# The probabilities of 16 attention heads turned by VectorE in 32x32 blocks and through DRAM, with each head's output two heads behind its scores

## The chip, the core and the metric

One core of one Trainium2 chip runs the whole program in one launch. The metric is the device time of that launch in microseconds (us). TensorE (PE) multiplies, VectorE (DVE) and ScalarE (ACT) do the element work, GpSimd (POOL) takes a few sums, and SyncE (SP) issues every DMA, all on one queue.

## The reference, cut to what matters

Two layers over 512 tokens of width 1024 in float32: retention with 4 heads, then latent attention (MLA) with 16 heads. The change is in the second. The part of it that counts:

```python
q_cat = jnp.concatenate([q_abs, q_rope], axis=-1) * scale
k_cat = jnp.concatenate([c_kv, k_rope], axis=-1)
def attend(args):                                   # one block of 128 queries
    s = jnp.einsum('bqhc,bkc->bhqk', qb, k_cat)
    s = jnp.where(key_idx[None, :] <= q_idx[:, None], s, neg)
    pr = jax.nn.softmax(s, axis=-1)
    return jnp.einsum('bhqk,bkc->bqhc', pr, c_kv)
...
o = jnp.einsum('bshc,chd->bshd', o_lat, w_uv).reshape(B, S, MLA_WIDTH)
return (jax.nn.silu(gate) * o) @ w_out
```

The scores come out with queries on the partitions. The product with the values needs keys on the partitions, so every head's probabilities have to be transposed.

## The kernel before, in words

Everything lies with channels on the partitions and 512 tokens in the free dimension. Each factor of a product is split into a part `hi` (ACT casts it to fp32r, line 88) and a rest `lo` (DVE subtracts, line 89), and each product is three matmuls, hi·hi, hi·lo and lo·hi (`mm3`, lines 97 to 99). Weights arrive raw by DMA (`wraw`, line 109) and are split in the same way (`whi`, `wlo`), in four buffers each.

The loop over 16 MLA heads runs in four groups of four. For head h:

- `mla_scores`: for each of four blocks of 128 queries, five matmuls over 128, 256, 384 or 512 keys into one of four PSUM banks of the pool `s` (three of `hpack` halves, L97 to L99, and two of the rotary part, L580 and L581). A DVE operation (L584) adds the mask and takes the row minimum, ACT takes the exponential with its row sum (L586), DVE the reciprocal (L587) and the scaling (L588). All four blocks lie in one tile `sm`.
- `mla_qk(h+1)`: the next head's queries and keys, 18 and 6 matmuls of 512 columns with their weights, then split into `hpack`. The next scores read it.
- `finish(h-1)`, which is `mla_pv`: twelve matmuls of 512, 384, 256 and 128 columns (`o_mla`), three of each. DVE multiplies the result by the gate `gl`, which comes from DRAM (`ut`, L613), and it is split into `u`.
- `mla_probs`: ten transposes of 128x128 by TensorE (L598) into banks of the same pool `s`, each then split from PSUM by ACT and DVE into `pt`, four pieces a head.
- Once a group: the output projection of the group before (`out_proj`, 96 matmuls of 512) at the group's head 0, the rotary queries of the next group (`mla_rope_q`, 36 of 512) at head 1, its values (`mla_v`, 48 of 256) at head 2.

The order on each engine is made by a scheduler from the order of the program and the buffers of the pools (8 `tmp`, 4 `mm` banks, 4 `s` banks, 2 `qk` tiles, one `sm`, one `pt`). Each engine then works its own list strictly in order.

The change touches `mla_qk`, `mla_scores`, `mla_probs`, `mla_pv` and the loop over heads, and the places of some tiles in memory.

Of the kernel before, what the change touches and what calls it, by code (L numbers as in the profile page):

```python
# [34 lines left out]
PTW = 1664  # L35
# [15 lines left out]
def trunk(ctx, tc, x, p, pos, gains, invf, rmask, smask, ret_in, ret_out, mla_in, uqk, uq_r, uv,  # L51
# [89 lines left out]
    dve.tensor_scalar(gn_h, g_sb[:, GN:GN + 16], 0.5, None, op0=ALU.mult)  # L141

# [136 lines left out]
    def ret_qk(h, i):  # L279
        acc = [mm_bank(), mm_bank()]  # L280
        for m in range(2):
            proj(acc[m], weights(ret_in[12 * h + 2 * i + m], KC, P), xg)
        pack = sb.tile([P, 2, 2, T], F32R, tag="qk", bufs=2, name="qkpack")
        d1, d2 = tmp("rot1"), tmp("rot2")
        rope_pair(acc[0], acc[1], cos_r, sin_r, d1, d2)
        split(pack[:, 0, 0], pack[:, 1, 0], d1)
        split(pack[:, 0, 1], pack[:, 1, 1], d2)
        return pack

    def ret_scores(h, q, k):  # L290
# [4 lines left out]
        at = sb.tile([P, 2 * PTW + 256], F32R, tag="pt", bufs=1, name="at")  # L295
        for j in range(TC):
            i0, n = IST[j], T - IST[j]
            js = slice(j * P, (j + 1) * P)
            s = s_bank("s_ret")
            for c in range(2):  # L300
                mm3(s[:, :n], (k[:, 0, c, js], k[:, 1, c, js]), (q[:, 0, c, i0:], q[:, 1, c, i0:]), c == 0, c == 1)
            a = tmp("a")
            off = h % 2 * 640 + 128 + i0 - j * P
            dve.tensor_tensor(a[:, :n], s[:, :n], masks[0][:, off:off + n], op=ALU.mult)
            at0 = 384 * j + i0
            split(at[:, at0:at0 + n], at[:, PTW + at0:PTW + at0 + n], a[:, :n])
        return at

    def ret_pv(h, at, v, gs):

        ssq = None
        for m in range(4):
            vs = slice(m * P, (m + 1) * P)
            o = mm_bank("o_ret")
            for j in range(TC):
                i0, n, at0 = IST[j], T - IST[j], 384 * j + IST[j]
                mm3(o[:, i0:], (v[0][:, j, vs], v[1][:, j, vs]),
                    (at[:, at0:at0 + n], at[:, PTW + at0:PTW + at0 + n]), j == 0, j == TC - 1)
            ssq = sum_squares(ssq, o, dve if m == 3 else pool)
            dve.tensor_tensor(gs[:, m], o, gs[:, m], op=ALU.mult)  # L320
        r = rstd_columns(ssq, RV)
        ut = big("u")
        u = [(ut[:, m], ut[:, 4 + m]) for m in range(4)]

        def normed():
            row = rstd_rows(r, "gn_row")
            for m in range(4):
                t = tmp("ut")
                dve.scalar_tensor_tensor(t, gs[:, m], gn_h[:, h * 4 + m:h * 4 + m + 1], row, op0=ALU.mult,
                                         op1=ALU.mult)  # L330
# [84 lines left out]
    rbc0 = rstd_rows(r0, "rbc0", "rbc")  # L415
    gs = ret_gate(0)
# [151 lines left out]

    def mla_scores(hh, pack, qs):

        sm = sb.tile([P, 1280], F32, tag="sm", bufs=1, name="sm")
        st = sb.tile([P, 3, TC], F32, tag="st", bufs=2, name="st")
        segs = []
        for i in range(TC):
            n = (i + 1) * P
            w_ = n
            qi = slice(i * P, (i + 1) * P)
            s = s_bank("s_mla")
            mm3(s[:, :w_], (pack[:, 0, qi], pack[:, 1, qi]), (pack[:, 2, :w_], pack[:, 3, :w_]), True, False)
            pe.matmul(s[:, :w_], qs[:, hh, qi], kr_hi[:, :w_], start=False, stop=False)  # L580
            pe.matmul(s[:, :w_], qs[:, hh, qi], kr_lo[:, :w_], start=False, stop=True)  # L581
            seg = sm[:, seg_at[i]:seg_at[i] + n]
            segs.append(seg)
            dve.tensor_tensor_reduce(seg, s[:, :n], smask_sb[:, T - n:], q_scale[:, i:i + 1], 3e38, ALU.add, ALU.min,  # L584
                                     st[:, 0, i:i + 1])
            act.activation(seg, seg, AF.Exp, bias=st[:, 0, i:i + 1], scale=-1.0, accum_out=st[:, 1, i:i + 1])  # L586
            dve.reciprocal(st[:, 2, i:i + 1], st[:, 1, i:i + 1])  # L587
            dve.tensor_scalar(seg, seg, st[:, 2, i:i + 1], None, op0=ALU.mult)  # L588
        return segs

    def mla_probs(segs):

        pt = sb.tile([P, 2 * PTW + 256], F32R, tag="pt", bufs=1, name="pt")
        for i in range(TC):
            n = (i + 1) * P
            tp = s_bank("tp_p")
            for j in range(i + 1):
                pe.transpose(tp[:, j * P:(j + 1) * P], segs[i][:, j * P:(j + 1) * P], ident)  # L598
            src = tp[:, :n].rearrange("p (j f) -> p j f", f=P)
            split(query_blocks(pt, 0, i), query_blocks(pt, 1, i), src)  # L600
        return pt

    def mla_pv(h, pt, v, dst):
        o = mm_bank("o_mla")
        for j in range(TC):
            i0, n, a0 = IST[j], T - IST[j], 384 * j + IST[j]
            vs = slice(h % 2 * P, h % 2 * P + P)
            mm3(o[:, i0:], (v[:, j, vs], v[:, 4 + j, vs]), (pt[:, a0:a0 + n], pt[:, PTW + a0:PTW + a0 + n]),
# [4 lines left out]
        dve.tensor_tensor(ut, o, gl, op=ALU.mult)  # L613
# [8 lines left out]
    v = mla_v(0)  # L622
# [6 lines left out]
    u = pt = None  # L629
    ssq, add = y_squares()  # L630

    def finish(h):
# [11 lines left out]
        mla_pv(h, pt, vs[grp][hh // 2], u[hh])  # L644

    vs = [v]
    for h in range(MH):
        grp, hh = divmod(h, 4)
        segs = mla_scores(hh, pack, qs)
# [11 lines left out]
        if h in (MH - 3, MH - 2):  # L661
            out_proj(mla_out[8:12], u_prev, y1, (hh,))
        if hh == 1 and grp < 3:
            qs_next = mla_rope_q(grp + 1)
        if hh == 2 and grp < 3:
            vs.append(mla_v(grp + 1))
# [97 lines left out]
```

## Time and profile before

| | |
|---|---|
| median of 3 runs | 1006.53 us (1005.63 to 1006.87) |
| the profiled execution | 1006.76 us, of which the span is 1005.0 and 1.8 lie around it |
| PE busy | 989.6 us of the span, 98% |
| DVE, ACT, POOL busy | 635.7, 413.2 and 68.4 us (63%, 41%, 7%) |
| granted TensorE clock | 1.00 in every stretch of the span |
| the loop over MLA heads | 629.9 to 923 us of the span |

Matmuls are pipelined: one starts before the one ahead has ended, so the time that a matmul takes from PE is read from start to start in the timeline, not from its duration. DVE's operations overlap too, by some 0.07 to 0.10 us. A share of an engine over the whole span says little about one stretch, so the windows over a stretch stand beside it.

### The profile page before, as it was taken

Reading aid. Unit: us, or ns where it says so; the run is one execution under the profiler, and the core shown is the slowest. Engines: PE = TensorE matmul, PEld = TensorE weight load, DVE = VectorE, ACT = ScalarE, POOL = GpSimd, SP = SyncE. Lnnn points to the kernel's source line nnn. Section 1 sums busy time; section 2 is a strip of 40 time slices with the busy share of each in tenths; the row PEclk is TensorE's granted clock in tenths of the full one; section 3 lists DMA queues with packets and bytes.
Section 4 is the critical chain, followed back from the end, with each engine's and each line's share of the span. In section 5 each row is a group of like instructions: output and inputs, shape, how many; then the busy total and the mean of one; then the engine's idle time right before and its main releaser. Section 6 shows DMA issues by size and latency. Waiting matters only on the chain.

```text
span 1005.0 us, 12505 instructions
## 1 busy us (share of the span) xinstructions
PE 989.6 (98%) x4780; PEld 828.6 (82%) x4780; DVE 635.7 (63%) x1062; ACT 413.2 (41%) x683; POOL 68.4 (7%) x54
## 2 busy tenths in 40 slices
PE   6999999999999999999999999999999999999998
PEld 4888888888888888877888888898888889888777
DVE  5776558455645567587664455777377568775583
ACT  6332334333223334555433233655445246444441
POOL 3000100010001002302130000000000000000400
PEclk9999999999999999999999999999999999999999
DMA  6433222412322232444334445342323224221431
GB/s 241 152 86 103 64 84 85 131 63 84 104 84 63 84 89 85 150 139 160 92 94 136 134 136 153 114 135 68 90 75 116 85 76 124 84 99 60 138 103 52
DMA packets 37547, 105.96 MB, mean 105 GB/s; under 512 B 5104, under 2 KB 5872, under 8 KB 37488
## 3 DMA queue, kind: packets, MB, share of 16 engines
q1 hardware_dynamic: 37488, 105.17, 33.9%
q8 instruction: 37, 0.61, 0.2%
q14 instruction: 22, 0.18, 0.1%
HBM read 92.57 MB, written 8.39 MB: 100 GB/s over the span
## 4 chain that ended last, share of the span: by engine, by line
PE 92%; DVE 3%; issue 2%; ACT 1%; DMA 1%; SPq 0%; POOL 0%; POOLq 0%; DVEq 0%; ACTq 0%
PE acc L98 20%; PE acc L99 20%; PE acc L97 20%; PE gate L98 6%; PE gate L99 6%; PE gate L97 6%; PE tp_p L598 1%; PE s_mla L97 1%; PE o_ret L99 1%; PE s_mla L581 1%; PE o_ret L98 1%; PE s_mla L99 1%; PE s_mla L580 1%; PE s_mla L98 1%; PE o_ret L97 1%
## 5 line engine op out<-in xcount | busy, mean ns | idle before, releaser
L88 ACT CAST whi<-wraw 128x1024 fp32r<-128x1024 f32 (+2 forms) x156 | 159.8, 1025 | 343.9 <-PE acc L98 145.7
L89 DVE TENSOR_TENSOR wlo<-wraw,whi 128x1024 fp32r<-128x1024 f32 (+2 forms) x156 | 187.9, 1206 | 89.7 <-ACT whi L88 89.6
L152 POOL TENSOR_TENSOR ssq<-ssq,sq 128x512 f32<-128x512 f32 x38 | 56.3, 1482 | 836.0 <-ACT sq L151 430.5
L97 PE MATMUL gate<-xg_hi,whi 128*128 128x512 f32 x256 | 101.1, 395 | 6.9 <-ACT whi L88 5.6
L98 PE MATMUL gate<-xg_lo,whi 128*128 128x512 f32 x256 | 100.8, 395 | 2.1 <-DVE xg_lo L92 2.1
L99 PE MATMUL gate<-xg_hi,wlo 128*128 128x512 f32 x256 | 100.4, 393 | 0.1
L97 PE MATMUL acc<-u,whi 128*128 128x512 f32 x240 | 93.9, 392 | 0.0
L98 PE MATMUL acc<-u,whi 128*128 128x512 f32 x240 | 93.6, 391 | 0.0
L99 PE MATMUL acc<-u,wlo 128*128 128x512 f32 x240 | 93.5, 390 | 0.0
L97 PE MATMUL acc<-xg_hi,whi 128*128 128x512 f32 x200 | 78.2, 391 | 0.3 <-ACT xg_hi L91 0.3
L98 PE MATMUL acc<-xg_lo,whi 128*128 128x512 f32 x200 | 78.0, 390 | 0.3 <-DVE xg_lo L92 0.3
L99 PE MATMUL acc<-xg_hi,wlo 128*128 128x512 f32 x200 | 77.9, 389 | 0.0
L97 PE MATMUL acc<-c_hi,whi 128*128 128x512 f32 x176 | 69.2, 393 | 0.0
L251 DVE TENSOR_TENSOR g<-gate,rbc 128x512 f32<-128x512 f32 x32 | 22.0, 690 | 74.0 <-PE gate L99 74.0
L99 PE MATMUL acc<-c_hi,wlo 128*128 128x512 f32 x176 | 68.8, 391 | 0.0
L98 PE MATMUL acc<-c_lo,whi 128*128 128x512 f32 x176 | 68.7, 390 | 0.0
L346 DVE TENSOR_TENSOR y<-acc,y 128x512 f32<-128x512 f32 x48 | 33.1, 691 | 51.2 <-PE acc L99 51.2
L97 PEld LDWEIGHTS gate<-xg_hi,whi 128*128 128x128 f32 x256 | 48.4, 189 | 18.1 <-ACT whi L88 6.3
L98 PEld LDWEIGHTS gate<-xg_lo,whi 128*128 128x128 f32 x256 | 48.4, 189 | 14.0 <-DVE xg_lo L92 4.1
L99 PEld LDWEIGHTS gate<-xg_hi,wlo 128*128 128x128 f32 x256 | 48.4, 189 | 10.3 <-DVE wlo L89 0.4
L98 PEld LDWEIGHTS acc<-u,whi 128*128 128x128 f32 x240 | 45.1, 188 | 9.8 <-DVE u L89 0.5
L97 PEld LDWEIGHTS acc<-u,whi 128*128 128x128 f32 x240 | 45.1, 188 | 9.3
(195 smaller groups left out, 2074.9 us busy)
## 6 DMA issues: line engine op xcount, KB each, us to landing
wraw<-in_ret_in SPq DMA_DIRECT2D x47, 512.0 KB, 3.6
wraw<-in_mla_in SPq DMA_DIRECT2D x25, 512.0 KB, 3.7
wraw<-in_ret_out SPq DMA_DIRECT2D x16, 512.0 KB, 3.6
wraw<-in_ple_g SPq DMA_DIRECT2D x16, 512.0 KB, 3.6
wraw<-in_uqk SPq DMA_DIRECT2D x16, 512.0 KB, 3.8
wraw<-in_mla_out SPq DMA_DIRECT2D x16, 512.0 KB, 3.7
gs_dram<-gsl SPq DMA_DIRECT2D x16, 256.0 KB, 4.1
qs<-rq SPq DMA_DIRECT2D x64, 64.0 KB, 2.0
```

The source lines that it names most:

```text
L88: act.copy(hi, src)
L89: dve.tensor_tensor(lo, src, r32(hi), op=ALU.subtract)
L97: pe.matmul(acc, ah, bh, start=first, stop=False)
L98: pe.matmul(acc, ah, bl, start=False, stop=False)
L99: pe.matmul(acc, al, bh, start=False, stop=last)
L152: (eng or pool).tensor_tensor(acc, acc, sq, op=ALU.add)
L251: dve.tensor_tensor(g, acc, rbc, op=ALU.mult)
L346: dve.tensor_tensor(y[:, c], acc, y[:, c], op=ALU.add)
L580: pe.matmul(s[:, :w_], qs[:, hh, qi], kr_hi[:, :w_], start=False, stop=False)
L581: pe.matmul(s[:, :w_], qs[:, hh, qi], kr_lo[:, :w_], start=False, stop=True)
L598: pe.transpose(tp[:, j * P:(j + 1) * P], segs[i][:, j * P:(j + 1) * P], ident)
```

## The change

`mla_scores` no longer keeps its blocks in `sm`: each block has a tile of the pool `tmp` (`seg`), and after the scaling DVE transposes each 128x128 piece in 32x32 blocks (ten STREAM_TRANSPOSE of 128x4x32 a head) into `tr`, which now has the one buffer of `sm`. `mla_fetch` stores `tr` (640 KB) to DRAM and loads it back with four DMAs of 32 partitions each (160 KB), which puts the blocks in their places, into `raw`, one buffer. `mla_probs` splits `raw` from SBUF in two pieces instead of four from PSUM. The queries of a head now lie as 4x32 interleaved pieces: the matmuls of `mla_pv` write `oq[:, :, 32j:]`, four pieces of up to 128 columns, and the multiplication by the gate puts them in natural order. TensorE's ten transposes a head are gone.

The output of a head comes two heads behind (`finish(h-2)`) and its probabilities one behind. `mla_v` moves to the group's head 0 for that group, `out_proj` to head 1, and the pieces of the last ones go behind the last scores. The retention's `at` and the heads' `hpack` lie elsewhere: `at` is packed to 1280 columns, and halves of `hpack` and `qkpack` start 64 columns apart from a multiple of 512; three unused tiles (`pad`) shift what follows them.

```diff
     def ret_qk(h, i):
...
-        pack = sb.tile([P, 2, 2, T], F32R, tag="qk", bufs=2, name="qkpack")
+        pack = sb.tile([P, QK], F32R, tag="qk", bufs=2, name="qkpack")
+        pack = pack[:, i * 64:i * 64 + 4 * T].rearrange("p (a c t) -> p a c t", a=2, c=2)
...
     def mla_qk(h):
-        pack = sb.tile([P, 4, T], F32R, tag="qk", bufs=2, name="hpack")
+        flat = sb.tile([P, QK], F32R, tag="qk", bufs=2, name="hpack")
+        pack = [flat[:, at:at + T] for at in (0, T, 2 * T + 64, 3 * T + 64)]
...
     def mla_scores(hh, pack, qs):
...
-        sm = sb.tile([P, 1280], F32, tag="sm", bufs=1, name="sm")
+        tr = sb.tile([P, 4, NS // 4], F32, tag="sm", bufs=1, name="tr")
...
-            seg = sm[:, seg_at[i]:seg_at[i] + n]
+            seg = tmp("seg")
...
-            dve.tensor_scalar(seg, seg, st[:, 2, i:i + 1], None, op0=ALU.mult)
+            dve.tensor_scalar(seg[:, :n], seg[:, :n], st[:, 2, i:i + 1], None, op0=ALU.mult)
             for j in range(i + 1):
-                pe.transpose(tp[:, j * P:(j + 1) * P], segs[i][:, j * P:(j + 1) * P], ident)
-            src = tp[:, :n].rearrange("p (j f) -> p j f", f=P)
-            split(query_blocks(pt, 0, i), query_blocks(pt, 1, i), src)
+                at = 32 * (JST[j] + i - j)
+                dve.transpose(tr[:, :, at:at + 32], seg[:, j * P:(j + 1) * P].rearrange("p (b k) -> p b k", k=32))
+        return tr
+
+    def mla_fetch(h, tr):
+
+        sp.dma_start(pt_dram[h], tr)
+        raw = sb.tile([P, 4, NS // 4], F32, tag="ptraw", bufs=1, name="raw")
+        for b in range(4):
+            sp.dma_start(raw[b * 32:(b + 1) * 32], pt_dram[h, :, b].rearrange("(a k) f -> k a f", k=32))
+        return raw
+
+    def mla_probs(raw):
+
+        pt = sb.tile([P, 2, 4, NS // 4], F32R, tag="pt", bufs=1, name="pt")
+        for at in (slice(0, 128), slice(128, NS // 4)):
+            split(pt[:, 0, :, at], pt[:, 1, :, at], raw[:, :, at])
         return pt
 
     def mla_pv(h, pt, v, dst):
         o = mm_bank("o_mla")
+        oq = o.rearrange("p (a q) -> p a q", a=4)
         for j in range(TC):
-            i0, n, a0 = IST[j], T - IST[j], 384 * j + IST[j]
+            at = slice(32 * JST[j], 32 * (JST[j] + TC - j))
...
-            mm3(o[:, i0:], (v[:, j, vs], v[:, 4 + j, vs]), (pt[:, a0:a0 + n], pt[:, PTW + a0:PTW + a0 + n]),
+            mm3(oq[:, :, 32 * j:], (v[:, j, vs], v[:, 4 + j, vs]), (pt[:, 0, :, at], pt[:, 1, :, at]),
...
     for h in range(MH):
...
+        if hh == 0:
+            vs.append(mla_v(grp))
         if h == MH - 1:
-            out_proj(mla_out[8:12], u_prev, y1, (3,))
-            ple = ple_proj(1, ple_input(1))
+            out_proj(mla_out[8:12], u_prev, y1, (1,))
+        if h > 1:
+            finish(h - 2)
         if h:
-            finish(h - 1)
-        pt = mla_probs(segs)
-        if hh == 0 and grp:
+            pts[h - 1] = mla_probs(raw)
+        raw = mla_fetch(h, tr)
+        if hh == 1 and grp:
...
+    ple = ple_proj(1, ple_input(1))
+    out_proj(mla_out[8:12], u_prev, y1, (2,))
+    finish(MH - 2)
+    pts[MH - 1] = mla_probs(raw)
+    out_proj(mla_out[8:12], u_prev, y1, (3,))
     next(ple)
     finish(MH - 1)
```

What the scheduler makes of it. On PE, from the end of head 3's pass to head 4's scores (`o_mla` is an output, of head 2 before and of head 1 in the change; `acc<-c_hi` is the projection for head 5; `s_mla` are head 4's scores), before:

```order
L99 MATMUL o_mla<-pt,v_4613 128x128
L598 MATMUL tp_p<-ident,sm 128x128 x10
L97 MATMUL acc<-c_hi,whi 128x512
L98 MATMUL acc<-c_lo,whi 128x512
L97 MATMUL s_mla<-hpack 128x128
L98 MATMUL s_mla<-hpack 128x128
L99 MATMUL s_mla<-hpack 128x128
```

and in the change:

```order
L106 MATMUL o_mla<-pt,v_4871 128x4x32
L104 MATMUL s_mla<-hpack 128x128
L104 MATMUL s_mla<-hpack 128x256
L104 MATMUL s_mla<-hpack 128x384
L104 MATMUL s_mla<-hpack 128x512
L104 MATMUL acc<-c_hi,whi 128x512
L105 MATMUL acc<-c_lo,whi 128x512
L106 MATMUL acc<-c_hi,wlo 128x512
L104 MATMUL acc<-c_hi,whi 128x512
L105 MATMUL acc<-c_lo,whi 128x512
L105 MATMUL s_mla<-hpack 128x128
L106 MATMUL s_mla<-hpack 128x128
```

The transposes are gone; the four hi·hi products of the scores, which need no `lo` of `hpack`, and five matmuls of the next projection now stand ahead of the first product that reads the `lo` of the keys.

On DVE, in head 3 (tile numbers tell heads apart: `hpack_5375` before and `hpack_5307` in the change are head 4's queries and keys), before:

```order
L588 TENSOR_SCALAR sm_5333<-sm_5333,st_5334 128x384
L587 RECIPROCAL st_5334<-st_5334 128x1
L588 TENSOR_SCALAR sm_5333<-sm_5333,st_5334 128x512
L89 TENSOR_TENSOR hpack_5375<-acc_5382,hpack_5375 128x512
L89 TENSOR_TENSOR wlo_5645<-wraw_5643,whi_5644 128x1024
L89 TENSOR_TENSOR hpack_5375<-acc_5403,hpack_5375 128x512
L613 TENSOR_TENSOR ut1_5427<-o_mla_5412,gl_5425 128x512
L89 TENSOR_TENSOR pt_5431<-tp_p_5432,pt_5431 128x128
```

and in the change (`hpack_5430` is head 5's, `raw_5246` head 2's probabilities, `o_mla_5344` head 1's output):

```order
L602 STREAM_TRANSPOSE tr_5251<-seg_5271 128x4x32 x2
L599 TENSOR_SCALAR seg_5284<-seg_5284,st_5252 128x384
L598 RECIPROCAL st_5252<-st_5252 128x1
L96 TENSOR_TENSOR hpack_5307<-acc_5335,hpack_5307 128x512
L602 STREAM_TRANSPOSE tr_5251<-seg_5284 128x4x32 x3
L599 TENSOR_SCALAR seg_5298<-seg_5298,st_5252 128x512
L96 TENSOR_TENSOR wlo_5690<-wraw_5688,whi_5689 128x1024
L602 STREAM_TRANSPOSE tr_5251<-seg_5298 128x4x32 x4
L96 TENSOR_TENSOR hpack_5430<-acc_5437,hpack_5430 128x512
L96 TENSOR_TENSOR pt_5363<-raw_5246,pt_5363 128x4x128
L632 TENSOR_TENSOR ut1_5359<-o_mla_5344,gl_5357 128x512
```

The second `lo` half of head 4's `hpack` now stands behind the reciprocal of the 512-key block, and the last four transposes, the multiplication by the gate and the split of head 2's probabilities around a projection of head 5. On ACT the exponentials of the 384- and 512-key blocks, which stood ahead of both copies of `hpack`, now stand behind them, with a weight cast between the two. On SP each head now has `gl`, the store of `tr` (it waits for DVE's last transpose), two weight loads, and the four loads into `raw` (they wait for the store to land and for the readers of `raw`), in this order.

## Rows read from the trace of the kernel before

**Rows 1.** The page's first part: span; busy us, share and instructions by engine.

```profile
span 1005.0 us, 12505 instructions
...
PE 989.6 (98%) x4780; PEld 828.6 (82%) x4780; DVE 635.7 (63%) x1062; ACT 413.2 (41%) x683; POOL 68.4 (7%) x54
```

**Rows 2.** Windows: stretch, us, busy PE, PEld, DVE, ACT, POOL, clock, DMA share, GB/s.

```profile
629.90:923.00 293.10, 292.73 (x1589) 254.72 (x1588) 201.33 (x474) 144.82 (x306) 0.00 (x0) 1.00 0.31 95
660.00:677.30 17.30, 17.30 (x116) 15.99 (x115) 15.54 (x36) 10.40 (x22) 0.00 (x0) 1.00 0.49 154
```

**Rows 3.** PE's timeline, 689 to 701: start, duration, engine, line, operation, tiles.

```profile
689.12 0.40 PE L98 MATMUL acc<-c_lo,whi 128*128 128x512 f32 x1
689.63 0.33 PE L97 MATMUL s_mla<-hpack 128*128 128x128 f32 x1
...
692.93 0.39 PE L99 MATMUL acc<-c_hi,wlo 128*128 128x512 f32 x1
...
697.72 0.40 PE L99 MATMUL acc<-c_hi,wlo 128*128 128x512 f32 x1
697.95 0.39 PE L97 MATMUL o_mla<-pt,v 128*128 128x512 f32 x1
...
699.81 1.28 PE L598 MATMUL tp_p<-ident,sm 128*128 128x128 f32 x10
700.85 0.47 PE L97 MATMUL acc<-u,whi 128*128 128x512 f32 x1
```

**Rows 4.** The chain of waits, 684 to 690: start, us, what.

```profile
688.10 0.68 DVE hpack L89
688.78 0.60 DVE ut L613
```

**Rows 5.** DVE groups by form, 629.9 to 923: busy us, mean ns | idle before.

```profile
L89 DVE TENSOR_TENSOR wlo<-wraw,whi 128x1024 fp32r<-128x1024 f32 x32 | 39.2, 1223 | 21.1 <-ACT whi L88 21.1
L89 DVE TENSOR_TENSOR hpack<-acc,hpack 128x512 fp32r<-128x512 f32 x30 | 20.6, 686 | 16.4 <-ACT hpack L88 16.4
...
L587 DVE RECIPROCAL st<-st 128x1 f32<-128x1 f32 x64 | 9.8, 159 | 4.4 <-ACT sm L586 4.0
...
L89 DVE TENSOR_TENSOR pt<-tp_p,pt 128x256 fp32r<-128x256 f32 x16 | 6.6, 415 | 0.0
...
L89 DVE TENSOR_TENSOR wlo<-wraw,whi 128x768 fp32r<-128x768 f32 x5 | 4.8, 958 | 8.5 <-ACT whi L88 8.5
...
L588 DVE TENSOR_SCALAR sm<-sm,st 128x128 f32<-128x128 f32 x16 | 4.4, 278 | 0.1
```

**Rows 6.** DVE's timeline, one head's softmax, 691 to 696.

```profile
691.49 0.34 DVE L584 CUSTOM_DVE_ANT_0 sm<-s_mla,smask_sb,q_scale 128x128 f32<-128x128 f32 x1
...
695.08 0.17 DVE L587 RECIPROCAL st<-st 128x1 f32<-128x1 f32 x1 [0.35 <-ACT sm L586]
695.28 0.49 DVE L588 TENSOR_SCALAR sm<-sm,st 128x512 f32<-128x512 f32 x1
```

**Rows 7.** ACT groups by form, 629.9 to 923.

```profile
L88 ACT CAST whi<-wraw 128x1024 fp32r<-128x1024 f32 x32 | 33.7, 1053 | 46.9 <-PE acc L98 42.0 <-issue 4.9
...
L586 ACT ACTIVATE sm<-sm,st 128x512 f32<-128x512 f32 x16 | 11.6, 726 | 8.2 <-DVE st L584 8.2
L586 ACT ACTIVATE sm<-sm,st 128x384 f32<-128x384 f32 x16 | 9.9, 618 | 5.6 <-DVE st L584 5.6
```

**Rows 8.** PE groups by form, 629.9 to 923.

```profile
L97 PE MATMUL s_mla<-hpack 128*128 128x256 f32 x16 | 5.3, 333 | 0.0
...
L98 PE MATMUL s_mla<-hpack 128*128 128x256 f32 x16 | 4.4, 277 | 0.0
```

**Rows 9.** The view of DMA issues: count, KB each, median us from issue to landing.

```profile
gs_dram<-gsl SPq DMA_DIRECT2D x16, 256.0 KB, 4.1
...
masks<-in_rmask SPq DMA_DIRECT2D x2, 640.0 KB, 5.1
```

**Rows 10.** SP's timeline, 744 to 755: sixteen loads in one row.

```profile
744.87 10.02 SPq L534 DMA_DIRECT2D qs<-rq  x16
```

More of the change, by code (lines that the diff above doesn't have):

```diff
@@ L33 @@
 IST = (0, 128, 256, 384)
-PTW = 1664
+JST = (0, 4, 7, 9)
+NS = 1280
+QK = 4 * T + 128
 WG = 1024
@@ L61, in trunk, with pad @@
     gs_dram = dr.tile([MH, P, T], F32, name="gs_dram")
+    pt_dram = dr.tile([MH, P, 4, NS // 4], F32, name="pt_dram")
+    def pad(name, n):
+        sb.tile([P, n], F32, name=name)
     def r32(ap):
@@ L294, in ret_scores @@
             sp.dma_start(masks[0], rmask[h // 2])
-        at = sb.tile([P, 2 * PTW + 256], F32R, tag="pt", bufs=1, name="at")
+        if h == 0:
+            pad("pad_pt", 64)
+        at = sb.tile([P, 2, NS], F32R, tag="pt", bufs=1, name="at")
         for j in range(TC):
@@ L304, in ret_scores @@
             dve.tensor_tensor(a[:, :n], s[:, :n], masks[0][:, off:off + n], op=ALU.mult)
-            at0 = 384 * j + i0
-            split(at[:, at0:at0 + n], at[:, PTW + at0:PTW + at0 + n], a[:, :n])
+            at0 = JST[j] * P
+            split(at[:, 0, at0:at0 + n], at[:, 1, at0:at0 + n], a[:, :n])
         return at
@@ L415, in trunk @@
     rbc0 = rstd_rows(r0, "rbc0", "rbc")
+    pad("pad_g8", 120)
     gs = ret_gate(0)
@@ L560, in mla_qk @@
         proj(acc, wq, cq)
-        split(pack[:, 0], pack[:, 1], acc)
+        split(pack[0], pack[1], acc)
         acc = mm_bank()
         proj(acc, lambda c, i, m: wq(6 + c, i, m), ckv)
-        split(pack[:, 2], pack[:, 3], acc)
+        split(pack[2], pack[3], acc)
         return pack
-    seg_at = (0, 128, 384, 768)
     def mla_scores(hh, pack, qs):
-        sm = sb.tile([P, 1280], F32, tag="sm", bufs=1, name="sm")
+        tr = sb.tile([P, 4, NS // 4], F32, tag="sm", bufs=1, name="tr")
@@ L589, in mla_scores @@
[L589 to L596, printed above, removed]
-            for j in range(i + 1):
-                pe.transpose(tp[:, j * P:(j + 1) * P], segs[i][:, j * P:(j + 1) * P], ident)
-            src = tp[:, :n].rearrange("p (j f) -> p j f", f=P)
-            split(query_blocks(pt, 0, i), query_blocks(pt, 1, i), src)
+            mm3(s[:, :n], (pack[0][:, qi], pack[1][:, qi]), (pack[2][:, :n], pack[3][:, :n]), True, False)
@@ new lines, in mla_scores @@
+            pe.matmul(s[:, :n], qs[:, hh, qi], kr_hi[:, :n], start=False, stop=False)
+            pe.matmul(s[:, :n], qs[:, hh, qi], kr_lo[:, :n], start=False, stop=True)
+            seg = tmp("seg")
+            dve.tensor_tensor_reduce(seg[:, :n], s[:, :n], smask_sb[:, T - n:], q_scale[:, i:i + 1], 3e38, ALU.add,
+                                     ALU.min, st[:, 0, i:i + 1])
+            act.activation(seg[:, :n], seg[:, :n], AF.Exp, bias=st[:, 0, i:i + 1], scale=-1.0,
+                           accum_out=st[:, 1, i:i + 1])
@@ L612, in mla_pv @@
         ut = tmp("ut1")
[L613 removed]
+        natural = lambda t: t.rearrange("p (i a q) -> p i a q", i=TC, a=4)
+        dve.tensor_tensor(natural(ut), o.rearrange("p (a i q) -> p i a q", i=TC, a=4), natural(gl), op=ALU.mult)
         split(*dst, ut)
@@ L621, in trunk @@
     qs = mla_rope_q(0)
-    v = mla_v(0)
     pack = mla_qk(0)
@@ L628, in trunk @@
     y1 = big("y1", F32)
-    u = pt = None
+    u, vs, pts, raw = None, [], {}, None
     ssq, add = y_squares()
@@ L643, in finish @@
             u += [(ut[:, m], ut[:, 2 + m]) for m in range(2)]
[L644 to L646 removed]
+        mla_pv(h, pts[h], vs[grp][hh // 2], u[hh])
     for h in range(MH):
         grp, hh = divmod(h, 4)
[L649 removed]
+        tr = mla_scores(hh, pack, qs)
         if h + 1 < MH:
             pack = mla_qk(h + 1)
+        if hh == 0:
+            vs.append(mla_v(grp))
         if h == MH - 1:
[L653 to L654 removed]
+            out_proj(mla_out[8:12], u_prev, y1, (1,))
+        if h > 1:
+            finish(h - 2)
         if h:
[L656 to L658 removed]
+            pts[h - 1] = mla_probs(raw)
+        raw = mla_fetch(h, tr)
+        if hh == 1 and grp:
             u_prev = u
             out_proj(mla_out[4 * (grp - 1):4 * grp], u, y1, range(4) if grp < 3 else (0,), first=grp == 1)
[L661 to L662 removed]
         if hh == 1 and grp < 3:
             qs_next = mla_rope_q(grp + 1)
[L665 to L666 removed]
         if hh == 3 and grp < 3:
             qs = qs_next
+    ple = ple_proj(1, ple_input(1))
[3 more added lines that the diff above has]
+    out_proj(mla_out[8:12], u_prev, y1, (3,))
     next(ple)
```

17 lines of the change are left out of this document (3 added, 14 removed).

## The prediction, made before the run

> **What bounds the kernel now.** First the shares: PE is busy 98% of the span, DVE 63% [rows 1]. Then the windows, since the change works between 629.9 and 923: there PE is busy 292.7 of 293.1 us at clock 1.00, DVE 201.3 and ACT 144.8 [rows 2]. PE is the bound, and what leaves PE comes off the time as long as no other engine then makes PE wait. DVE comes next, and its 69% is an average: in its fullest stretch, 17.3 us from 660, it is busy 15.54 us, 90% [rows 2]. PE's timeline gives the true price of its work, from start to start, and the one place where it waits: after 689.12 a matmul of 512 columns should pass in 0.23, but the next starts 0.51 later, at 689.63 [rows 3], a wait of 0.28. The chain of waits names the cause: DVE makes a `lo` half of `hpack`, then the gated output, and PE follows [rows 4]. This stands at the end of three groups' third heads, 0.85 us in all. The profiled execution took 1006.76, 0.2 above the median of 1006.53; the sum below starts from the former.
>
> **What PE loses.** A head's ten transposes take PE from 699.81 to 700.85 [rows 3], 1.04 us; 16 heads make **16.6 us**, all of it on the path.
>
> **What PE does in a head.** Scores 689.63 to 692.93, 3.30; a projection matmul (697.95−692.93)/22 = 0.228, so 24 take 5.48; the output 697.95 to 699.81, 1.86 [rows 3]. Together 10.64 us without the transposes. The places of `hpack` may also help a little: of two matmuls of the same form, that on the `hi` keys is 56 ns longer than that on the `lo` keys [rows 8]; 16 of them make 0.9. With the like in other forms I bound this by 0 and 2 us and take **0.5**.
>
> **What DVE gets.** Splitting four pieces from PSUM becomes two from SBUF, of 512 and 768 elements. The nearest rows, 686 and 958 ns [rows 5], less 0.08 of overlap each, give 1.48 us a head. New are ten transposes of 128 elements a partition. No row shows one. The cheapest small operation is a reciprocal of one element, 159 ns; a row that surely does more is a split of 256 elements, 415 ns. The nearest in work is the scaling of 128 elements from SBUF, 278 ns [rows 5], 0.20 from start to start. I take **0.20**, 2.0 us a head, and keep 0.15 to 0.42, 1.5 to 4.2 a head. The Trainium skill (VectorE: DVE Perf Modes, The three transpose paths) gives 311 ns for a 128x128 bf16 transpose on VectorE and 390 on TensorE, and advises TensorE where its result may go to PSUM; by that an operation would come every 0.23, 0.3 a head more, and the sum below would be between nothing and 3.6 us worse (1.2 in each of three groups).
>
> The softmax of a head runs from 691.49 to 695.77 with 0.35 idle [rows 6], 3.85 us. Two `hpack` halves at 0.61, the gated output and its split at 0.61 each (all like the 686 ns row) make 2.44. With 1.48 and 2.0 a head costs DVE **9.77 us** against PE's 10.64: it fits, barely. But PE's list has heads 2 to 5 with little beside them: four heads, 42.6, and `mla_v`, 48 matmuls of half the columns at 0.12, 5.8, together 48.4 us. DVE has there 39.1, the splits of `v` (four at 0.61, 2.4) and six weight splits at 1.15 (1223 ns less 0.08 [rows 5]), 6.9: also 48.4. Two full engines that feed each other can't both run without waits.
>
> **The wait that takes the place.** I walk head 3 to head 4, with zero where PE starts head 3's scores. The projection's first accumulator is ready at 3.3 + 18 × 0.228 = 7.4, the second at 8.8. ACT copies both by about 9.5, then does the 384-key exponential (618 ns and the row sum, 0.8), a weight cast (1053 ns) and the 512-key exponential (726 and 0.19) [rows 7], which end at 10.3, 11.35 and 12.3. DVE's reciprocal, 12.4, stands ahead of the second `lo` half in its list, so that half is ready at 13.1. PE, after 10.64, does the four hi·hi products of the next scores (0.63) and five matmuls of the next projection (1.14), and wants the half at 12.4: it waits 0.7. Walked alike: 0.95 from head 2 to 3; 1.4 from 4 to 5, where DVE's list holds the splits of head 2's probabilities and the gated output behind a projection of head 5, so that the mask of the last block, and with it a bank of `s`, comes late; 0.6 in head 5's output projection, which wants `u` of head 3. That is **3.65 a group**, three groups, and 0.95 from head 14 to 15: 11.9, of which I leave 0.6 to slack in the output projection of the third group, which is cut in pieces: **11.3**. The 0.85 of today goes, since those heads' ends are walked anew: **+10.4**.
>
> **Edits at nothing.** ACT has less to cast (two pieces for four) and has 148 us idle in the stage [rows 2]. The store of 640 KB takes about the 5.1 us of the masks' load, at least the 4.1 of 256 KB [rows 9]; the four loads cost SP 4 × 0.63 (10.02/16 [rows 10]) and land some 4 later. From a head's last transpose, some 14 us after its scores began, store (5.1), loads (2.5 to issue, 4 to land) and split (1.5) end at 27; its output starts at 2 × 10.64 + 8.8 = 30. SP stands at the store until DVE's last transpose and at the loads until the store has landed, and the next weights stand behind both; they are loaded a head ahead of use, with four buffers. `tr` has one buffer: the next head's first transpose waits until the store has read it. I walk 5.6 to 6.2 us between a head's last transpose and the next one's first, against 0.4 + 5.1. Thin, hence a rival below. After head 15 PE has 22 us of output projection, gate and head 14's output ahead of the last output, which needs 17: covered. If it were not, 2 to 4 us would show once.
>
> **Sum.** 1006.8 − 16.6 − 0.5 + 10.4 = 1000.1, so **1000.0 us**, by itself 995 to 1004.5.
>
> **Rivals.**
> - *The waits are covered.* The scheduler's list lets PE run ahead by a projection (24 × 0.228) and a delay of one head may be made up in the next; for it speaks that today's DVE, 90% full, costs PE 0.85 us only [rows 2, 3], against it the equal sums of 48.4. Then 1006.8 − 16.6 − 0.5 = 989.7, with up to 2 for the places of the tiles 988.2. Chance 0.28.
> - *DVE becomes the bound: slower.* If a transpose comes every 0.42, as for 256 elements [rows 5], a head costs 2.2 more; four heads 8.8, of which DVE's idle time beside my waits takes 3.6, leaves 5.2 a group, 15.7 and once 2.2 more: 1018. The tie is where 40(c − 0.20) − 3.6 a group, three times, and 10(c − 0.20) once make 6.7: c = 0.34. For it: the operation moves columns to partitions, which no row does, and a scaling of 128 is the best case. Against it: it has one SBUF input and few elements. Chance 0.17, a third of it within 0.2% of today.
> - *The output's matmuls write in pieces.* They write PSUM as four pieces of 96, 64 or 32 columns, nine of twelve with gaps; those nine take 1.86 − 3 × 0.23 = 1.17 us a head today [rows 3]. Twice that would add 18.7: 1018.8. No matmul of the trace writes with gaps, so the trace neither shows nor excludes it. The Trainium skill (SBUF — State Buffer, the box on SBUF cachelines) says that non-contiguous PSUM access slows matmuls much, as PSUM's lines hold two fp32 values; runs of 32 columns and more cross a line no more often than one long run, so I give the case little: chance 0.04.
> - *The store comes late.* If it lands 6.5 after its issue instead of 5.1, DVE stands about 1 us at ten heads' first transposes, with reciprocals and `hpack` halves behind; hidden in part, +6: 1006. Chance 0.06.
>
> **How the numbers follow.** Forecast 0.45, covered 0.28, DVE dear 0.17, pieces 0.04, store late 0.06. A measurement of this kernel can tell 0.2%, 2 us, from no change: 1004.5 to 1008.5 count as the same. Faster: 0.45 + 0.28 = 0.73. Same: 0.06 and a third of 0.17, 0.12. Slower: the rest, 0.15. The range runs from the covered case, 988.5, to the dear transpose as far as c = 0.36, 1010; outside stay about 0.03 below and 0.13 above.
>
> **What would show it.** 160 STREAM_TRANSPOSE on DVE, from start to start near 0.20; no matmul of `tp_p`; PE's idle time before `s_mla` on `hpack` released by DVE, 0.5 to 1.5 us at the ends of heads 2, 3 and 4 of each group and none in the output projections' bulk; DVE in heads 2 to 5 busy over 95%; output matmuls still 0.23, 0.17, 0.13 and 0.11 apart; no wait of DVE on the store of `tr`. I am wrong if the transposes come over 0.34 apart, if ACT waits for the loads into `raw`, or if PE stays over 99% busy through the dense heads.

## The result and the profile after

The changed kernel takes **995.38 us** (median of 4 runs, 995.32 to 996.77), against 1006.61 for the kernel before in the same session: a ratio of 0.9893 with a 95% interval of 0.9881 to 0.9905, 11.2 us less. Predicted were 1000.0 (988.5 to 1010) and 0.73 for faster. The direction was right, the size too small: 6.5 us forecast, 11.2 measured.

The first part of the page answers to [rows 1]:

```profile
span 993.5 us, 12481 instructions
...
PE 973.0 (98%) x4620; PEld 812.3 (82%) x4620; DVE 658.2 (66%) x1190; ACT 405.0 (41%) x651; POOL 68.4 (7%) x54
```

The span is 11.5 us shorter. PE is busy 16.6 us less and idle 5.1 more (20.5 against 15.4), so part of what was gained came back as waits. The 16.6 is not the price of the transposes alone: it also holds what the tiles' places gave (run 1), and a 512-column matmul counts as busy for 0.39 us but passes in 0.23, so the first part of each wait counts as busy too. DVE gained 128 instructions and 22.5 us. Now DVE's groups in the MLA loop (operation, shape, count | busy us, mean ns | idle before):

```profile
L602 DVE STREAM_TRANSPOSE tr<-seg 128x128 f32<-128x128 f32 x160 | 37.0, 280 | 0.1
L96 DVE TENSOR_TENSOR pt<-raw,pt 128x768 fp32r<-128x768 f32 x16 | 15.2, 948 | 0.0
L96 DVE TENSOR_TENSOR pt<-raw,pt 128x512 fp32r<-128x512 f32 x16 | 10.8, 675 | 0.8 <-ACT pt L95 0.8
```

A block transpose takes 280 ns, the same as the scaling of as many elements, 278 [rows 5]. From start to start it is 0.20 us, as DVE's timeline in head 2 shows: four transposes take 0.81 us to the start of the next operation, three take 0.61.

```profile
664.57 0.68 DVE L602 STREAM_TRANSPOSE tr<-seg 128x128 f32<-128x128 f32 x3
665.18 0.44 DVE L599 TENSOR_SCALAR seg<-seg,st 128x512 f32<-128x512 f32 x1
...
666.14 0.88 DVE L602 STREAM_TRANSPOSE tr<-seg 128x128 f32<-128x128 f32 x4
666.95 1.51 DVE L96 TENSOR_TENSOR pt<-raw,pt 128x512 fp32r<-128x512 f32 x2
```

(37.0 / 160 = 0.23 is more, since it counts the last transpose of every run in full, with the part that overlaps the next operation. The expectations of runs 2 and 9 below use that 0.23.) The transpose almost never waits: 0.1 us idle in front of 160 of them, so `tr`'s single buffer holds nobody up. The windows over heads 2 to 5 show where DVE's new work bites (columns as in [rows 2]):

```profile
654.70:665.20 10.50, 10.50 (x58) 9.21 (x56) 10.25 (x31) 6.71 (x14) 0.00 (x0) 1.00 0.26 65
665.20:676.50 11.30, 10.83 (x59) 9.28 (x58) 8.90 (x27) 5.10 (x12) 0.00 (x0) 1.00 0.80 240
676.50:689.80 13.30, 13.27 (x83) 11.74 (x82) 9.48 (x28) 6.64 (x15) 0.00 (x0) 1.00 0.64 194
689.80:711.30 21.50, 20.55 (x109) 17.52 (x108) 21.50 (x63) 11.62 (x25) 0.00 (x0) 1.00 0.66 184
```

DVE is idle 3.8 of 13.3 us in the third stretch and then full, 21.5 of 21.5, in the fourth, where PE waits most. DVE's timeline at the seam shows why (the bracket is the idle time before and who ended it):

```profile
680.46 0.88 DVE L602 STREAM_TRANSPOSE tr<-seg 128x128 f32<-128x128 f32 x4
684.93 0.69 DVE L96 TENSOR_TENSOR hpack<-acc,hpack 128x512 fp32r<-128x512 f32 x1 [3.59 <-ACT hpack L95]
685.54 0.68 DVE L96 TENSOR_TENSOR pt<-raw,pt 128x512 fp32r<-128x512 f32 x1
686.13 0.68 DVE L632 TENSOR_TENSOR ut<-o_mla,gl 128x512 f32<-128x512 f32 x1
```

ACT's timeline at the same place:

```profile
684.31 0.59 ACT L95 CAST hpack<-acc 128x512 fp32r<-128x512 f32 x1 [6.66 <-PE acc L106]
684.79 1.36 ACT L95 CAST pt<-raw 128x512 fp32r<-128x512 f32 x2
```

and SP's, with the store of head 2 and its loads:

```profile
668.65 0.40 SPq L607 DMA_DIRECT2D pt_dram<-tr  x1
...
672.98 1.75 SPq L610 DMA_DIRECT2D raw<-pt_dram  x4
```

The loads into `raw` for head 2 are issued from 672.98 to 674.73 and land some 4 us after the last issue (the median of these loads is 4.0 us), before 680. ACT, with nothing to do from 677.7, and DVE from 681.3 both stand at a copy of head 5's projection, which PE finishes at 684.3. The split of `raw`, the gated output and its split are ready and queue behind it; DVE does them when the next head's masks are due as well. PE's timeline has the bill at the same place:

```profile
689.78 0.58 PE L104 MATMUL s_mla<-hpack 128*128 128x128 f32 x3
690.68 0.49 PE L104 MATMUL s_mla<-hpack 128*128 128x512 f32 x1 [0.32 <-DVE st L594]
691.80 0.38 PE L104 MATMUL acc<-whi,c_hi 128*128 128x256 f32 x1 [0.62 <-DVE hpack L96]
```

From start to start these two gaps cost 0.54 and 1.00 us beyond the matmuls' own time, the second with 0.10 for the slower start of the matmul behind it. In the first PE waits for a bank of `s` that DVE's mask still reads, in the second `mla_v`, which reads no `hpack`, waits for the accumulator bank that DVE's subtraction for `hpack` still reads. Counted so, all gaps over 0.25 us in the loop are: heads 2 to 3 and 3 to 4 of the first group 0.69 and 0.30; the groups' first heads (4, 8, 12) 1.54, 2.17 and 1.41; 0.28 and 0.34 elsewhere; 0.57 before head 15's scores; 1.57 in front of the last output. Together 8.9, where before there were 0.85. Those at heads 4, 8 and 12 are 5.1 of it.

### The profile page after: what moved, and what is told of

Read it like the earlier page. It is cut to its first block, busy times and chain, and to the rows that moved or that the text cites. A ratio compares the mean times of both kernels' runs of the same rounds, so it can differ in the third digit from the quotient of the medians.

```text
span 993.5 us, 12481 instructions
## 1 busy us (share of the span) xinstructions
PE 973.0 (98%) x4620; PEld 812.3 (82%) x4620; DVE 658.2 (66%) x1190; ACT 405.0 (41%) x651; POOL 68.4 (7%) x54
## 4 chain that ended last, share of the span: by engine, by line
PE 88%; DVE 6%; issue 2%; ACT 2%; DMA 1%; SPq 0%; POOL 0%; POOLq 0%; DVEq 0%; ACTq 0%
PE acc L105 20%; PE acc L104 19%; PE acc L106 19%; PE gate L105 6%; PE gate L106 6%; PE gate L104 6%; PE s_mla L105 1%; PE o_ret L105 1%; PE o_ret L106 1%; PE o_ret L104 1%; PE s_mla L106 1%; PE s_mla L592 1%; PE s_mla L591 1%; PE o_mla L105 1%; PE o_mla L106 1%
## 5 line engine op out<-in xcount | busy, mean ns | idle before, releaser
L106 PEld LDWEIGHTS acc<-u,wlo 128*128 128x128 f32 x240 | 45.1, 188 | 9.4
L105 PEld LDWEIGHTS acc<-u,whi 128*128 128x128 f32 x240 | 45.1, 188 | 9.4 <-DVE u L96 0.2
```

The costliest lines, as they stand in the source:

```text
L105: pe.matmul(acc, ah, bl, start=False, stop=False)
L106: pe.matmul(acc, al, bh, start=False, stop=last)
```

## The experiments

Theory A: the gain is the ten transposes off PE's path, and what comes back is made by the order of ACT's and DVE's lists, which put work that is ready behind a copy that isn't. Rival B: by DVE's load. Rival C: by the trip through DRAM. A further question was the price of the tiles' places. Medians are compared with the changed kernel's 995.38; ratios, where given, are to the kernel before, whose medians were 1006.34 to 1006.61 in every session. In some runs the granted clock fell after waits of PE. What that cost is estimated from the mean granted clock of the profiled span, as the part of the span that is missing from full speed: 1.0 us for the changed kernel (0.999 of 993.5).

**1. The places of the tiles undone.**

```diff
-QK = 4 * T + 128
+QK = 4 * T
...
-    pad("pad_ssq", 104)
...
-        pack = pack[:, i * 64:i * 64 + 4 * T].rearrange("p (a c t) -> p a c t", a=2, c=2)
+        pack = pack[:, 0:4 * T].rearrange("p (a c t) -> p a c t", a=2, c=2)
...
-            pad("pad_pt", 64)
...
-    pad("pad_g8", 120)
...
-        pack = [flat[:, at:at + T] for at in (0, T, 2 * T + 64, 3 * T + 64)]
+        pack = [flat[:, at:at + T] for at in (0, T, 2 * T, 3 * T)]
```

> The changed kernel with hpack and qkpack back at multiples of 512 columns and the three unused tiles taken out; nothing else differs. Theory A (the gain is the ten transposes off TensorE, less new waits of PE on DVE; the places of the tiles are worth about 1 us): 996 to 997 us, and the hi*hi and rotary score matmuls a few ns longer from start to start. Rival B (the places carry a good part of the 11 us gained): 999 us or more.

Measured 998.46 (996.68 to 999.38, 5 runs), ratio 0.9919 (0.9905 to 0.9932); span 995.4 against 993.5. So the places are worth 1.9 us by the profiled spans, 3.1 by the medians; this kernel's runs spread with a granted clock of 0.997 to 1.000. PE is busy 975.8 us here, only 13.8 less than before:

```profile
PE 975.8 (98%) x4620; PEld 811.9 (82%) x4620; DVE 658.3 (66%) x1190; ACT 404.9 (41%) x651; POOL 68.3 (7%) x54
```

It isn't `hpack`: the pair of [rows 8] is unmoved by the places (the product on the `lo` keys took 277 ns before and takes some 309 with either places). In the changed kernel, with the 64-column offsets:

```profile
L105 PE MATMUL acc<-x_lo,whi 128*128 128x512 f32 x120 | 46.3, 393 | 0.5 <-DVE x_lo L96 0.5
...
L104 PE MATMUL acc<-x_hi,whi 128*128 128x512 f32 x120 | 44.8, 391 | 0.4 <-ACT x_hi L95 0.4
L104 PE MATMUL s_mla<-hpack 128*128 128x256 f32 x16 | 5.3, 334 | 0.0
L105 PE MATMUL s_mla<-hpack 128*128 128x256 f32 x16 | 5.0, 309 | 0.0
```

and with the places undone:

```profile
L105 PE MATMUL acc<-x_lo,whi 128*128 128x512 f32 x120 | 46.7, 396 | 0.3 <-DVE x_lo L96 0.3
L104 PE MATMUL acc<-x_hi,whi 128*128 128x512 f32 x120 | 45.4, 396 | 0.3 <-ACT x_hi L95 0.3
L104 PE MATMUL s_mla<-hpack 128*128 128x256 f32 x16 | 5.3, 333 | 0.0
L105 PE MATMUL s_mla<-hpack 128*128 128x256 f32 x16 | 4.9, 308 | 0.0
```

The gate matmuls of the two tails, on `x_hi` and `x_lo`, take 3 to 5 ns less each with the places as changed: 360 of them, 1.4 us. Whether the unused tiles or the offsets do it was not taken apart. The median lies between what the two theories expected: the places carry more than A said, but 2 to 3 of the 11 us, not most of them.

**2. Every block transpose twice.**

```diff
-                dve.transpose(tr[:, :, at:at + 32], ...)
+                for _ in range(2):
+                    dve.transpose(tr[:, :, at:at + 32], ...)
```

> Every block transpose of VectorE is issued twice, so a head costs DVE ten more at 0.23 us, 2.3 us. From head 2 to head 6 of the first group the changed kernel has DVE busy about 50 of 57 us. Theory A (the waits that are left are PE waiting for DVE in the dense heads): four heads bring 9.2 us a group against some 6.5 of idle time, part of which the list can't use; three groups and one head more: 10 to 25 us slower, 1005 to 1020, with PE's waits on hpack, the gate and the masks' banks growing. Rival B (DVE has slack, the waits come from the trip through DRAM): at most 3 us slower, below 999.

Measured 1005.25 (10 runs), ratio 0.9984 (0.9975 to 0.9993): 9.9 us slower than the changed kernel, the mild end of theory A, for 30.1 us more on DVE (busy 688.3 us against 658.2; 160 more at 0.20 make 32). DVE was busy 55.0 of 59 us from 656 to 715, and the granted clock stayed at 1.00. DVE's load matters, at about a third of its amount.

**3. Splits of the probabilities ahead of the projection's copy.**

```diff
-    def mla_qk(h):
+    def mla_qk(h, after=None):
...
-        split(pack[0], pack[1], acc)
+        if after:
+            with tc.issue_after(after[0].ins), tc.issue_after(after[1].ins):
+                split(pack[0], pack[1], acc)
+        else:
+            split(pack[0], pack[1], acc)
```

> The changed kernel, but at the first head of a group the split of the earlier head's probabilities is put ahead of the copy of the next projection's first half, on ACT and on DVE. In the changed kernel both engines stand idle 3 to 3.6 us at that place, for a projection, with the loaded probabilities behind it, and PE then waits 1.5, 2.2 and 1.4 us in heads 4, 8 and 12. Theory A (head-of-line: the order of the list, not DVE's capacity, makes these waits): they fall by half or more, 990.5 to 993. Rival B (DVE is simply full there, 21.5 of 21.5 us): within 1 us of 995.4. Rival C (the loads land later than the projection): ACT waits for the load and it is slower, 996 to 999.

Measured 1002.16 (5 runs), 6.8 us slower, and for none of the three reasons. The splits did run early (DVE at 681.1), but ACT's list now had the cast of `u` behind the copies of the projection, and DVE and the masks behind that: the same fault in another place, as DVE's timeline shows.

```profile
683.09 0.34 DVE L598 CUSTOM_DVE_ANT_0 seg<-s_mla,smask_sb,q_scale 128x128 f32<-128x128 f32 x1
...
686.60 0.69 DVE L96 TENSOR_TENSOR u<-ut,u 128x512 fp32r<-128x512 f32 x1 [3.15 <-ACT u L95]
```

ACT does wait 2.60 us for the load there, as rival C has it, but ends the split before the projection is ready. PE's waits grew, with one of 2.1 us at each of heads 8 and 12, and the granted clock fell after heads 4 and 8; its mean, 0.996 of 1000.4 us, makes some 3 of the 6.8 us, an estimate.

**4. Loads that don't wait for the store.**

```diff
-            sp.dma_start(raw[b * 32:(b + 1) * 32], pt_dram[h, :, b]...)
+            src = rmask[0].rearrange("p (b f) -> p b f", b=4)
+            sp.dma_start(raw[b * 32:(b + 1) * 32], src[:, b]...)
```

> The loads into raw read a constant table of the same size in DRAM and so don't wait for the store of the transposed probabilities; the store is still made. The attention uses that table in place of the probabilities. Theory A (the trip through DRAM is covered by the lag of two heads, except after the last head): PE's waits in the groups stay, only the 1.6 us before the last head's output go: 993.5 to 995.5. Rival C (store and load set the waits in heads 2 to 5 too): those go as well, below 992.

Measured 991.94 (4 runs), ratio 0.9857 (0.9843 to 0.987): theory A missed. The waits at heads 4, 8 and 12 shrank to 0.55 each, and the one before the last output, which A gave to the trip, stayed. This looked like rival C, but the edit had also changed the lists: since the loads no longer depend on the store, the scheduler put the splits of `pt` and of `u` ahead of the projection's copies by itself. Run 5 takes the two apart.

**5. That order with the real loads.** At each group's first head both halves of the next projection's split, the values' splits and the later weights are held behind what is ready:

```diff
+            pack = mla_qk(h + 1, (list(last), [exps[1]]) if h and hh == 0 else ((), ()))
...
+            late = [exps[3]] if h else []
+            vs.append(mla_v(grp, late))
```

(`last` holds the last splits of `u` and `pt`, `exps` the exponentials.)

> The same question as the run that put only the split of the probabilities ahead and was slower: there ACT's cast of u fell behind the projection's copies, and DVE and PE behind it. Here, at the first head of groups 1 to 3, all that is ready stands ahead: split of the probabilities, split of u, then the first half of the next projection, the exponentials, the second half, the values; real loads. It is nearly the list that the run with free loads had by itself. Theory A (order of the lists): 991.5 to 993, the waits at heads 4, 8 and 12 down to about 0.6 each. Rival C (the trip through DRAM sets them): ACT waits for the loads, 995 or more.

Measured **992.52** (992.3 to 992.82, 4 runs), ratio 0.9861 (0.9845 to 0.9877): 2.9 us below the changed kernel and the best version of this study. The trip through DRAM was not the limit; the order was. ACT's timeline at the same seam as above:

```profile
679.33 1.36 ACT L101 CAST pt<-raw 128x512 fp32r<-128x512 f32 x2 [1.40 <-DMA raw<-pt_dram]
682.83 0.62 ACT L101 CAST u<-ut 128x512 fp32r<-128x512 f32 x1 [2.15 <-DVE ut L641]
684.58 0.59 ACT L101 CAST hpack<-acc 128x512 fp32r<-128x512 f32 x1 [1.13 <-PE acc L112]
```

and DVE's:

```profile
681.54 0.65 DVE L102 TENSOR_TENSOR pt<-raw,pt 128x512 fp32r<-128x512 f32 x1
...
683.58 0.69 DVE L102 TENSOR_TENSOR u<-ut,u 128x512 fp32r<-128x512 f32 x1
```

ACT splits at 679.33, as soon as the load has landed, instead of 684.79; DVE has done all of it by 684.2, where it used to begin. PE's gaps at heads 4 and 8 fell from 1.54 and 2.17 to 0.55 each; at head 12 they rose from 1.41 to 2.0, which was not followed up. The wait of 1.57 before the last output went too, as PE's list there now puts matmuls of the next projection between those of the output. Against that, PE now waits some 0.7 us at the end of each group's third head, and in the changed kernel only in the first group.

**6. The last head as well.** As run 5, with the third and fourth weight casts of the last projection behind the last split of `pt`.

```diff
+    out_proj(mla_out[12:16], u, y1, (0, 1), on_chunk=add)
+    with behind(last_pt):
+        out_proj(mla_out[12:16], u, y1, (2, 3), on_chunk=add)
```

> As the run before, and the casts of the last projection's third and fourth weights stand behind the split of the last head's probabilities. In the changed kernel and with free loads PE waits 1.6 us before the last head's output, and ACT holds that split behind a weight cast that waits for PE. Theory A: 1 to 1.6 us less than the run before, 990 to 992. Rival C (the last head's trip sets it): the same as the run before, within 0.5.

992.84 (4 runs), the same: run 5 had already lost that wait, with PE doing part of the next projection there, so this run had nothing left to show.

**7. `u`'s rest on GpSimd.** As run 6, and

```diff
-        last[:2] = split(*dst, ut)
+        last[:2] = (act.copy(dst[0], ut), pool.tensor_tensor(dst[1], ut, r32(dst[0]), op=ALU.subtract))
```

> As the run before, with the subtraction that makes u's lo part on GpSimd, which is idle there (its 128x512 sums take about 1.5 us each), and DVE 0.6 us a head lighter. Theory A (DVE close to full in the dense heads, but what is left of the waits, about 0.6 at four or five places, comes from the order of copy, exponential and lo half): 0 to 2 us less. Rival D (GpSimd and DVE slow each other on SBUF): slower by 1 us or more, DVE's operations longer.

995.59 (993.52 to 995.9, 4 runs): no gain, rather a loss. DVE's operations are not longer (block transposes 284 ns against 285 in run 6, the split of `raw` 954 against 955), so there is no sign of rival D. One gap of PE behind DVE's `hpack` at head 12 grew to 2.1 us. The profile is of the fastest execution, 993.52, at a granted clock of 0.999; the other three, 995.29 to 995.90, show 0.998, and where their time went isn't shown. Taking 0.6 us a head from DVE brought nothing.

**8. One head behind.**

```diff
-        if h > 1:
-            finish(h - 2)
         if h:
             pts[h - 1] = mla_probs(raw)
+            finish(h - 1)
         raw = mla_fetch(h, tr)
-        if hh == 1 and grp:
+        if hh == 0 and grp:
...
-    finish(MH - 2)
```

(So `out_proj` is back at head 0.)

> The changed kernel with a head's output one head behind its scores, and the output projection one head earlier, as before. Theory A (the lag covers store, loads and split): a head's loads land some 24 us after its scores began (head 2: 654.7 to about 679) and its split ends 2.5 later, while its output would come some 19 to 20 after: 5 to 8 us of PE waiting in the heads that have nothing else beside them, about nine, and less in the others: 1030 to 1090. Rival (DVE's order alone matters): below 1010.

1013.66 (2 runs), ratio 1.0071 (1.0051 to 1.0091): slower than before, as A said, but by much less than A's 1030 to 1090; why its waits are so much shorter was not looked into. The lag of a second head makes the change pay: without it the kernel takes 18 us more. Some 7 of them, an estimate, are the granted clock, 0.992 of 1010.4 us, which fell at three places.

**9. Four block transposes of ten.**

```diff
-            for j in range(i + 1):
+            for j in (i,):
```

> Only the four block transposes on the diagonal of each head are made; the other six places of tr hold zeros written once, so the attention is cut to the diagonal blocks. Store, loads and splits stay as they are, and so does the order at the first heads of the groups. DVE is 6 x 0.23 = 1.4 us a head lighter. Theory A (the order of the lists makes the waits at heads 4, 8 and 12): DVE still stands behind the next projection there, and most of the 5.1 us stay: 993 to 995.5. Rival B (DVE's load makes them): they go, 991 to 992.5.

999.9 (5 runs), 4.5 us slower with 16.6 us less on DVE (busy 641.6 against 658.2; 64 transposes, 18.5 us busy, for 160 and 37.0). Neither theory foresaw the number, but B is out: the waits at heads 4, 8 and 12 did not go with the load. At head 8 they were even longer, in another list, and the windows show what followed:

```profile
765.00:770.00 5.00, 4.91 (x38) 4.49 (x36) 4.09 (x6) 4.35 (x8) 0.00 (x0) 1.00 0.25 76
770.00:775.00 5.00, 2.30 (x7) 1.43 (x8) 5.00 (x22) 2.95 (x9) 0.00 (x0) 0.78 0.79 186
775.00:780.00 5.00, 5.00 (x23) 4.71 (x22) 3.50 (x6) 1.53 (x2) 0.00 (x0) 0.53 0.33 132
```

The mean granted clock, 0.996 of 998.6 us, makes some 3 of the 4.5 us, an estimate.

**10. TensorE's transposes beside VectorE's.**

```diff
+            tp = s_bank("tp_p")
             for j in range(i + 1):
...
+                pe.transpose(tp[:, j * P:(j + 1) * P], seg[:, j * P:(j + 1) * P], ident)
```

> TensorE makes its ten transposes a head again, into a bank that nobody reads, beside VectorE's. Theory A (each stands on the path at about 0.1 us): 16 x 1.04 = 16.6 us more, less what falls into today's waits and what moves because a bank of s is taken: 1005 to 1013. Rival (TensorE waited anyway, so they are hidden): below 1000.

1055.57 (4 runs): 60 us, not 17. Here the transposes stand on PE right behind the softmax of their own head, in the kernel before they had a projection and an output in between; PE waits 14.5 us for DVE's scaling in front of `tp_p` alone, and the clock falls again, to a mean of 0.990 over 1053.6 us. It says nothing of the 16.6 us. These rest on the trace before, where the 160 transposes take 16.5 us from start to start; no run takes the transposes alone off PE.

**11. The second half of `hpack` ahead of the weights' cast.** As run 5, with the weight casts of the groups' first heads behind the copy of the keys:

```diff
+        with behind(kv[0][:1] if h and h % 4 == 0 else ()):
+            wq = weights(uqk[h], 8, P)
```

> The best version so far (splits ahead at the groups' first heads, 992.5), and the weight casts of each group's next first head stand behind the copy of the second half of hpack, which ACT now does 0.8 us later than it could at head 3 of each group, where PE waits 0.7. Theory A: three or four such waits of 0.7 go, 990 to 991.5. Against it: the weight loads behind those casts come later, which may cost as much: 992 to 995.

995.96 (4 runs), 3.4 us slower than run 5: the weights came late (ACT waits 1.70 us for `wraw` at head 3, and the 512-key exponential and the second half of `hpack` stand behind), and PE waited for `hpack` in seven places, 4.2 us by the view of waits. The wait before the last output is back as well.

## Why the prediction was right, and where it was off

- **Transposes off PE, 16.6:** right. In the trace before, the 160 take 16.5 us from start to start, and they are gone. That PE's busy time fell by 16.6 as well, from 989.6 to 973.0, is chance: with the places undone it fell by 13.8.
- **The places, 0.5 of a bound of 2:** mis-sized. They gave 1.9 by the spans (3.1 by the medians), and not where the prediction looked: [rows 8] did not improve, the matmuls on `x_hi` and `x_lo` did. Added up from start to start without the waits and the transposes, PE's matmuls take 964.9 us before, 963.9 in run 1 and 961.3 in the changed kernel: 2.6 for the places (the spans show 1.9, as run 1's first matmul comes 0.3 earlier and its waits are 0.4 shorter), and 1.0 more that was not forecast and whose cause is open.
- **A block transpose, 0.20 out of 0.15 to 0.42:** right, 0.20 from start to start, 280 ns each. The Trainium skill (VectorE: DVE Perf Modes, The three transpose paths) gives 311 ns for 128x128 in bf16; the estimate of 0.23 from it is further off than the 0.20 from the rows. The Trainium skill's advice (VectorE: DVE Perf Modes, Rules for kernel authors) to leave a 128x128 transpose to TensorE where PSUM will do does not hold here: PE is the bound, and each one costs it 0.1 us.
- **The wait that takes the place, 11.3:** this step failed in size. It took one walk of the first group for all three, 3.65 each: 0.95, 0.7, 1.4 and 0.6. The walk found most of the places and the right engine, and the wait at heads 4, 8 and 12 was if anything too small (1.5, 2.2 and 1.4 against 1.4). But of these 5.1 us the late bank of `s`, which the walk named, makes about half; 2.7 are the wait of `mla_v` for its accumulator bank, which it had not. The others were 0.69, 0.30 and nothing in the first group, and less in the next two, whose lists differ: 2.5, 2.5 and 1.7 a group. Before head 15's scores 0.57 came instead of 0.95, and the last output, called covered, waited 1.57: ACT held the split of the probabilities behind a weight cast that waited for PE, and with free loads (run 4) that wait stayed. In all 8.9 instead of 11.3, net 8.0 instead of 10.4. That the totals lie so near is partly luck: without the last output's wait, which the walk put at nothing, it would be 7.3 instead of 11.3.
- **The sum:** 16.5 for the transposes, 2.6 for the places and the 1.0 of pace above come off, 8.0 of waits in the loop come back. That makes 12.1, and smaller waits, in the loop and outside it, take 0.6 of it back, to the 11.5 us between the spans. Of the 4.7 us that were forecast too few (6.5 for 11.2), about 2.4 lie in the waits, 2.1 in the places and 1.0 in the other pace, less those 0.6. The measured time is at the lower edge of the forecast case itself, 995 to 1004.5.
- **"Two full engines that feed each other can't both run without waits":** half right. The sum had DVE full from head 2 to 5, 48.4 of 48.4 us, and over 95% was to show it; it was busy 50.1 of 56.6 us, 89%, in the four windows above. DVE's load has a price (run 2), but the waits at the groups' first heads came from idle time that both lists held open: with DVE's work unchanged run 4 took two thirds of them away and run 5 those at heads 4 and 8, and run 9 kept them with four transposes of ten.
- **Covered at no cost:** store (3.5 us to landing, not 5.1) and loads (4.0) were covered by the lag; run 8 shows what the lag was for. ACT did wait for the loads twice, 1.71 us before 788.42 and 1.37 before 866.97, which the prediction counted as a sign of being wrong; no gap of PE over 0.25 us follows either.
- **Rivals.** *DVE dear*: its tie at 0.34 us a transpose was too near. With two of 0.20 in each place, 0.40, run 2 took 1005.25 and was still not slower than the kernel before; the formula gives 1000.1 + 3 × (40 × 0.20 − 3.6) + 10 × 0.20 = 1015. *Pieces in PSUM*: no. PE's timeline of one output, from its first matmul to the next head's scores:

```profile
674.61 0.39 PE L104 MATMUL o_mla<-pt,v 128*128 128x512 f32 x1
...
675.29 0.34 PE L104 MATMUL o_mla<-pt,v 128*128 128x384 f32 x1
...
676.46 0.45 PE L104 MATMUL s_mla<-hpack 128*128 128x128 f32 x2
```

  Twelve matmuls take 1.85 us, nine of them written in pieces, as against 1.86 [rows 3].
  The Trainium skill (SBUF — State Buffer, the box on cachelines) says that any non-contiguous access to PSUM slows matmuls much; for runs of 32 columns and more these rows show nothing of it. *Store late*: no, 0.1 us in all.

## What to carry to other kernels

When PE is the bound and its work moves to a second engine, price the new waits head by head from each engine's list, and look first for an engine that stands idle at a copy of unfinished work with finished work behind it: here that order was worth 2.9 us (waits went at heads 4 and 8 and at the last output and grew elsewhere), while taking load off DVE brought nothing (runs 7 and 9), though adding to it cost 9.9 us (run 2). Holding back one instruction moves the fault along the list (runs 3 and 11); hold back the whole group that is not ready. A trip through DRAM of some 10.5 us (from the store's issue at 668.82 to the split at 679.33 in run 5) costs next to nothing if a whole extra stage of lag covers it (run 5 is 0.6 us above run 4, whose loads don't wait), and 18 us if not, part of them by the clock.

## What the runs showed of the hardware

- After PE's waits had bunched up, the granted clock fell. In run 9 PE was busy 2.30 of the 5 us from 770 and the clock over the next 5 us was 0.53, close to the lower of its two levels, 1.2 of 1.2 and 2.4 GHz; in run 8 PE was busy 5.30 of 10 us, then 0.53 for 6 us of full work. The changed kernel, with 3.68 busy of the same 5 us, kept 1.00, and so did run 3 after 2.67 of the 5 us from 855. So a wait of PE can cost more than its own length, which none of the walks priced.
- Matmuls of one form took 391 or 396 ns, 228 or 232 from start to start, by where their operands lay, and only three unused tiles and 64-column offsets differed (run 1). What in the addresses does it was not tried.
- A block transpose of 128x128 in float32 came every 0.20 us on DVE, the same as a scaling of 128 elements, and issued twice in each place it stayed so (284 ns against 280, still 0.20 apart).
